# Second block's attention: low key parts and compressed values on all 128 rows, value products alternating by column half

## The chip, the core and the metric

The kernel runs on one core of one Trainium2 chip. The metric is the device time of one execution in microseconds (us). A core has five engines that run side by side and wait for each other through semaphores: PE (TensorE, matrix products; PEld is its weight load), DVE (VectorE), ACT (ScalarE), POOL (GpSimd) and SP, whose queue issues most of the loads. A matrix product has a stationary operand (the weights, up to 128 rows by 128 columns) and a moving operand of N columns that streams past it; the result goes to PSUM. A product may use a part of the array only: here "64\*128" in a row of the profile is a product on 64 rows of the array (a contraction over 64), "128\*64" one on all rows and one half of the columns (a result of 64 channels, in the lower or the upper half of the PSUM partitions), "32\*64" one on a quarter of the rows and half of the columns.

## The reference, cut to what matters

The kernel computes two blocks one after the other. The first (two layers of gated mixers and MLP, 512 tokens of x and 256 of a context) is the greater part of the time. The second block has eight heads of 64 channels in two groups, with three attentions per head that are added with gates: over compressed keys (31 of them), over selected blocks and over a window. With 512 tokens every block is selected and the window covers the sequence, so the last two are causal attentions with different keys and values. Four memory heads attend to 256 memory tokens beside them.

```python
s_c = einsum('bgrqd,bgnd->bgrqn', qb, k_c) * scale          # compressed
p_c = masked_softmax(s_c, c_mask); o_c = einsum('bgrqn,bgnd->bgrqd', p_c, v_c)
s_s = einsum('bgrqd,bgqkld->bgrqkl', qb, ks_g) * scale      # selected
o_s = einsum('bgrqkl,bgqkld->bgrqd', masked_softmax(s_s, s_mask), vs_g)
s_w = einsum('bgrqd,bgkd->bgrqk', qb, kw_blk) * scale       # window
o_w = einsum('bgrqk,bgkd->bgrqd', masked_softmax(s_w, w_mask), vw_blk)
o = gb[..., 0:1] * o_c + gb[..., 1:2] * o_s + gb[..., 2:3] * o_w
s_m = einsum('bshd,bmhd->bhsm', mq, mk) * scale             # memory
o_m = einsum('bhsm,bmhd->bshd', softmax(s_m), mv)
```

## The kernel before

Channels lie on the 128 partitions and tokens along the columns. Most products are made in a fast format (float32r) from numbers split in a high and a low part: high times high, plus the two mixed products. A product in full float32 (value products, transposes aside) is two passes of PE.

The program is recorded first. `Recorder` takes every instruction with the regions it touches; `schedule` (line 226) is a list scheduler that gives each engine its next instruction by priority (the place in the program) and readiness, by estimated durations (`cost`, line 191), and places the buffers; line 358 then issues everything in that order. So every row of the profile has the line L358, and instructions are told apart by the buffers they name: `pd` (projections), `pm` (scores, transposes) and `pa` (value products) are PSUM, with 3, 4 and 1 buffers; `slot` is a large SBUF row, `tmp` a scratch row, `wr`, `wh` and `wl` a loaded weight tile and its high and low parts, `const` what stays for good. The order on each engine is fixed when the program is built; on the chip an engine that waits holds up all that stands behind it.

The attention of the second block (`block2`, line 1570) comes after projections of keys, values and queries. A tile of queries `i` (0 to 3) holds two heads, one for each group `g`; head `g` has the rows 64g to 64g+63. `split_q` (line 1586) puts the high part of a head's queries on its own 64 rows and the low part on the other 64. The keys' high part `khi` is copied to both halves of the rows (ACT), so that one product of 128 rows gives high times high plus low times high. The keys' low part `klo` (line 1606) lies on the head's own 64 rows only.

A unit is (i, tb), tb being a block of 128 tokens; i = 0 to 3, tb = 3, 2, 1, 0. `nsa_scores` (line 1786) makes for each of two branches `br` and two groups `g`: a product with `khi` on 128 rows, a product with `klo` on 64 rows, and the causal mask added by a bf16 product with the identity, all of N = 512, 384, 256 or 256 columns (the mask 128); then DVE takes the maximum and ACT the exponential. `nsa_values` (line 1813) transposes each map in blocks of 128 (PE into `pm`), copies them to `tmp` (ACT for br 0, DVE for br 1), multiplies them with the values (`pa`, 128\*64, N = 128), and adds the compressed attention by one product per head with `vc`, which lies on 32 rows per token block (32\*64). One head is done before the other. Memory units (`mem_scores`, `mem_values`, lines 1842 and 1861) do the same for a pair of memory heads, with keys in `mem.khi` and `mem.klo` (line 1835, filled by `mem_keys`) and value products of N = 256. They stand after the second tile of queries. Between the units stand the projections and the output tiles of the list `beside` (line 1912): each is a stretch of 128\*128 products, `pd<-slot,wh` and `pd<-slot,wl`.

Before the attention the compressed keys and values are made: `psv` (line 1668) is a PSUM tile with the compressed values four times, once per quarter of the partitions, by 32-column products, and one ACT copy takes it to `vc`.

Elsewhere, `onesD` holds a matrix of 1/1024 and one of 1/256 for means (`csum`, `rstd`), the rope tables are loaded into a slot of their own (`rope_load`), and `mem_norm` (line 1544) loads the memory tokens into two slots.

Of the kernel before, what the change touches and what calls it, by code (L numbers as in the profile page):

```python
# [13 lines left out]
F32 = mybir.dt.float32  # L14
# [30 lines left out]
class View:  # L45
    """A region of a buffer that gets its place only when the order of the instructions is known."""
# [90 lines left out]
class Recorder:  # L137
    """Takes the program as it is written, orders each engine's instructions by priority and readiness with
    estimated durations, places the buffers, and then issues everything in that order."""
# [86 lines left out]
    def schedule(self):  # L226
        """List scheduling. A buffer's kind is served in program order."""
# [32 lines left out]
        def place(o):  # L260
            """places the buffers that the instruction is the first to touch, if they are all to be had"""
# [99 lines left out]
def tile_net(tc: tile.TileContext, A, out):  # L361
# [13 lines left out]
    def ld(o, i):  # L375
        sp.dma_start(out=o, in_=i)
# [28 lines left out]
    onesD = const([P, 2, P], F32)  # L405
    vec.memset(onesD[:, 0], 1.0 / 1024)
    vec.memset(onesD[:, 1], 1.0 / 256)
# [9 lines left out]
    def csum(srcs, n, w=0):  # L417
        """the mean over the channels of some blocks, on every partition"""
        ps = pm()[:, :n]
        for i, x in enumerate(srcs):  # L420
            pe.matmul(ps, onesD[:, w], x, start=i == 0, stop=i == len(srcs) - 1)
        return ps

    def rstd(ps, n):
        r = rst([P, TC])[:, :n]
        A_(r, ps, AF.Ln, bias=epst)
# [3 lines left out]
    def add_square(acc, o, sl, n, first):  # L430
        """adds the squares of a block to a tile of sums"""
# [51 lines left out]
    def run(blocks, acts, evac, order=R8, nk=None):  # L483
        """blocks: (key, source, groups); one weight tile after the other, all its tokens"""
# [5 lines left out]
    def narrow(src, acts, groups, evac):  # L490
        """a block of 32 columns: its high and low parts side by side, their products in two sets of rows"""
# [15 lines left out]
    def run_outer(blocks, acts, evac, groups, done=None, order=R8, ready=(), before=None):  # L507
        """as run, but group by group over a few resident weight tiles"""
# [55 lines left out]
    def pre(l, kind):  # L564
        """the gain and shift before the mixers (0) or the MLP (2), by conditioning"""
# [9 lines left out]
    def modulate(r, g, hs, gs, rs):  # L575
        """the next input of the matrix products: r * rs * gain + shift, in the two parts, r as four pairs of blocks"""
# [23 lines left out]
    def rms(r, n):  # L600
        ps = pm()[:, :n]
        for p in range(4):
# [3 lines left out]
            pe.matmul(ps, onesD[:, 0], q[:, 0], start=p == 0, stop=p == 3)  # L606
# [16 lines left out]
    def post_chain(g, o_, qs, old, hs, gs, gain=None):  # L623
        """the residual plus norm(o), kept in o's place and in DRAM, then the next norm"""
# [19 lines left out]
    def pairs():  # L644
        """activations in two parts: four tiles of [part, block of the pair, token]"""
# [26 lines left out]
    def rope_tables():  # L672
        """the cosines and signed sines by position, kept in DRAM until the second block"""
# [64 lines left out]
    def rows_of_three():  # L738
        """rows of the tokens of x, three to a slot"""
# [9 lines left out]
    class Later:  # L749
        """the tokens of x alone, by their place among all"""  # L750
# [7 lines left out]
    def gates(S, GX):  # L758
# [26 lines left out]
        # each head has two rows: the first of them takes the high part, the second the low one  # L785
# [46 lines left out]
    def mixers(l, hs, back, steps):  # L832
# [6 lines left out]
        # Fourier input and half of the conv module's  # L839
# [11 lines left out]
        # Fourier mixing: the sums over pairs of tokens s and n - s feed the cosines, the differences the sines,  # L851
# [1233 lines left out]
```

## Time and profile before

| | us |
|---|---|
| median of three runs | 2059.37 |
| lowest and highest of them | 2058.71, 2061.32 |
| the profiled execution, first to last instruction (span) | 2061.5 |

| engine | busy us | share of the span | instructions |
|---|---|---|---|
| PE | 1965.2 | 95% | 12772 |
| DVE | 1386.3 | 67% | 2380 |
| ACT | 878.3 | 43% | 1699 |
| POOL | 501.9 | 24% | 486 |

The span of the profiled execution is 2.1 us longer than the median of the runs, so the two agree within 0.1%. The attention with what runs beside it fills the stretch from 1785 to 2044 us of the span; the last 14 us finish the output. In the lists of the profile a matmul's duration contains its way through the array, which overlaps with the next one; what a product costs is the distance from its start to the next start.

### The profile page before, as it was taken

Reading aid. Unit: us, or ns where it says so; the run is one execution under the profiler, and the core shown is the slowest. Engines: PE = TensorE matmul, PEld = TensorE weight load, DVE = VectorE, ACT = ScalarE, POOL = GpSimd, SP = SyncE. Lnnn points to the kernel's source line nnn. Section 1 sums busy time; section 2 is a strip of 40 time slices with the busy share of each in tenths; the row PEclk is TensorE's granted clock in tenths of the full one; section 3 lists DMA queues with packets and bytes.
Section 4 is the critical chain, followed back from the end, with each engine's and each line's share of the span. In section 5 each row is a group of like instructions: output and inputs, shape, how many; then the busy total and the mean of one; then the engine's idle time right before and its main releaser. Section 6 shows DMA issues by size and latency. Waiting matters only on the chain.

```text
span 2061.5 us, 32412 instructions
## 1 busy us (share of the span) xinstructions
PE 1965.2 (95%) x12772; PEld 1672.1 (81%) x12772; DVE 1386.3 (67%) x2380; ACT 878.3 (43%) x1699; POOL 501.9 (24%) x486
## 2 busy tenths in 40 slices
PE   5999998988999999999899998899999998999999
PEld 3978885877988999999788886788989897776676
DVE  6588677287545665566878775887787785465664
ACT  4433355454322332234543355544343464553442
POOL 2210141245211222113320051542232232111210
PEclk8999998999999999999999999999999999999999
DMA  8233335251433221122321234322323342200201
GB/s 296 89 106 104 122 129 185 76 185 52 132 104 123 72 73 41 62 83 103 118 84 52 72 134 164 103 82 93 113 83 123 117 162 81 83 31 32 79 26 59
DMA packets 82570, 207.47 MB, mean 101 GB/s; under 512 B 8945, under 2 KB 36849, under 8 KB 82418
## 3 DMA queue, kind: packets, MB, share of 16 engines
q1 hardware_dynamic: 66690, 189.13, 27.0%
q10 hardware_dynamic: 15728, 16.27, 2.3%
q8 instruction: 100, 1.64, 0.3%
q14 instruction: 52, 0.43, 0.1%
HBM read 189.12 MB, written 16.25 MB: 100 GB/s over the span
## 4 chain that ended last, share of the span: by engine, by line
PE 65%; DVE 8%; issue 2%; ACT 1%; POOL 1%; DMA 1%; DVEq 0%; POOLq 0%; ACTq 0%
PE pd L358 44%; PE pm L358 18%; DVE slot L358 5%; PE pa L358 4%; DVE tmp L358 2%; DVE wl L358 1%; POOL slot L358 1%; ACT slot L358 0%; DMA wr<-in_w_ada 0%; ACT tmp L358 0%; ACT rs L358 0%; ACT wh L358 0%; DVE small L358 0%; POOL ftmp L358 0%; DMA wr<-in_w_in 0%
## 5 line engine op out<-in xcount | busy, mean ns | idle before, releaser
L358 PE MATMUL pd<-slot,wh 128*128 128x256 f32 (+2 forms) x4384 | 1092.2, 341 | 18.4 <-DVE slot L358 12.4
L358 PEld LDWEIGHTS pd<-slot,wh 128*128 128x128 f32 (+1 forms) x4384 | 745.1, 189 | 127.6 <-issue 18.7
L358 PE MATMUL pd<-slot,wl 128*128 128x256 f32 (+1 forms) x2136 | 724.1, 340 | 5.8 <-DVE wl L358 5.6
L358 PEld LDWEIGHTS pd<-slot,wl 128*128 128x128 f32 x2136 | 406.8, 191 | 55.0 <-DVE wl L358 7.7
L358 ACT ACTIVATE wh<-wr 128x1024 fp32r<-128x1024 f32 (+2 forms) x202 | 205.0, 1015 | 425.0 <-PE pd L358 388.1
L358 DVE TENSOR_TENSOR wl<-wr,wh 128x1024 fp32r<-128x1024 f32 (+2 forms) x199 | 248.4, 1248 | 129.1 <-ACT wh L358 128.2
L358 PE MATMUL pm<-slot,slot 128*128 128x256 f32 (+4 forms) x1674 | 256.7, 297 | 2.1 <-DVE tmp L358 1.6
L358 PEld LDWEIGHTS pm<-slot,slot 128*128 128x128 f32 (+1 forms) x1674 | 216.7, 191 | 28.2 <-issue 14.4
L358 DVE TENSOR_TENSOR slot<-pd,slot 128x512 f32<-128x512 f32 (+1 forms) x208 | 119.4, 574 | 127.0 <-PE pd L358 124.4
L358 PE MATMUL pd<-slot,slot 128*128 128x256 f32 (+1 forms) x1048 | 146.9, 289 | 2.9 <-ACT slot L358 2.6
L358 PEld LDWEIGHTS pd<-slot,slot 128*128 128x128 f32 x1048 | 132.8, 191 | 7.6 <-ACT slot L358 3.8
L358 DVE TENSOR_TENSOR slot<-ftmp,slot 128x512 fp32r<-128x512 f32 (+2 forms) x116 | 93.5, 809 | 36.1 <-POOL ftmp L358 34.5
L358 ACT ACTIVATE tmp<-tmp 128x512 f32<-128x512 f32 (+3 forms) x122 | 62.2, 545 | 126.9 <-DVE tmp L358 125.8
L358 DVE SCALAR_TENSOR_TENSOR slot<-slot,const,slot 128x512 f32<-128x512 f32 (+2 forms) x184 | 113.2, 664 | 0.8
L358 POOL TENSOR_TENSOR ftmp<-tmp 128x512 f32<-128x512 f32 x54 | 58.5, 1104 | 214.5 <-ACT tmp L358 214.5
L358 POOL TENSOR_TENSOR wr<-wr 128x512 f32<-128x512 f32 x27 | 39.3, 1455 | 290.0 <-DVE wl L358 248.9
L358 POOL TENSOR_TENSOR ftmp<-ftmp 128x256 f32<-128x256 f32 (+1 forms) x72 | 66.1, 918 | 166.7 <-ACT ftmp L358 162.5
L358 ACT ACTIVATE slot<-tmp 128x512 fp32r<-128x512 f32 (+1 forms) x134 | 80.7, 628 | 58.8 <-DVE tmp L358 38.8
L358 DVE TENSOR_TENSOR slot<-wr,slot 128x512 fp32r<-128x512 f32 (+1 forms) x85 | 87.3, 1033 | 17.2 <-ACT slot L358 17.2
L358 PE MATMUL pm<-slot,wh 128*128 128x256 f32 x544 | 98.4, 281 | 0.0
L358 ACT ACTIVATE slot<-wr 128x512 fp32r<-128x512 f32 (+1 forms) x85 | 72.0, 855 | 44.7 <-POOL wr L358 22.4
L358 PEld LDWEIGHTS pm<-slot,wh 128*128 128x128 f32 x544 | 84.0, 188 | 2.8 <-issue 1.6
(202 smaller groups left out, 2478.2 us busy)
## 6 DMA issues: line engine op xcount, KB each, us to landing
wr<-in_w_mlp SPq DMA_DIRECT2D x128, 512.0 KB, 3.4
wr<-in_w_ada SPq DMA_DIRECT2D x80, 512.0 KB, 4.0
wr<-in_w_in SPq DMA_DIRECT2D x66, 512.0 KB, 3.3
dram<-slot ACTq DMA_DIRECT2D x52, 256.0 KB, 2.5
tmp<-dram SPq DMA_DIRECT2D x40, 256.0 KB, 3.8
slot<-in_w_ada SPq DMA_DIRECT2D x16, 512.0 KB, 10.1
wr<-in_w_out SPq DMA_DIRECT2D x16, 512.0 KB, 3.9
wr<-in_w_out SPq DMA_DIRECT2D x8, 384.0 KB, 2.9
```

The costliest lines, as they stand in the source:

```text
L358: o.fn(*[conv(x) for x in o.a], **{k: conv(x) for k, x in o.k.items()})
```

## The change

The low parts of the keys get the same two copies as the high ones: `klo[g][br]` (and `mem.klo[h]`) is written on both halves of the rows, by two DVE subtractions instead of one, and the product with it is made on 128 rows. A third `kh` slot holds what this needs. The compressed values `vc` get one zero-padded tile of 128 rows per token block (`memset` once, four ACT copies of 32 rows instead of one copy of 128), and their product is made on 128 rows and 64 columns. In `nsa_values` the loop over branches is now the outer one, both heads' maps are transposed and copied, and then the products go block by block with the two heads in turn; both compressed products come last. `mem_values` alternates likewise. The copy that ACT makes is now that of head 0 and DVE's that of head 1.

To make room, `onesD` keeps only the 1/1024 matrix; the convolution module's mean of 256 channels takes it with a factor of 4 (in a `scalar_tensor_tensor` in place of a `tensor_tensor`, and in the scale of the logarithm), and the rope tables go to free columns of two slots that are in use anyway, by two loads of half the size. The rest of the diff removes comments.

```diff
@@ nsa keys (block2)
-        kh = [slot([P, 3, TX], F32R) for _ in range(2)]
+        kh = [slot([P, 3, TX], F32R) for _ in range(3)]
         khi = [[kh[g][:, br] for br in range(2)] for g in range(2)]
-        klo = [kh[br][:, 2] for br in range(2)]
+        klo = [[kh[2][:, br] if g else kh[br][:, 2] for br in range(2)] for g in range(2)]
         for br in range(2):
             for g in range(2):
-                a, b = own(g)
-                A_(khi[g][br][a], dst[br][a], AF.Copy)
-                A_(khi[g][br][b], dst[br][a], AF.Copy)
-                vec.tensor_tensor(klo[br][a], dst[br][a], khi[g][br][a].bitcast(F32), op=ALU.subtract)
+                a = own(g)[0]
+                for rows in own(g):
+                    A_(khi[g][br][rows], dst[br][a], AF.Copy)
+                    vec.tensor_tensor(klo[g][br][rows], dst[br][a], khi[g][br][a].bitcast(F32), op=ALU.subtract)
@@ compressed values
-        vc = const([P, 2, 64], F32)
-        A_(vc, psv, AF.Copy)
+        vc = const([P, 4, 2, 64], F32)
+        vec.memset(vc, 0.0)
+        for j in range(4):
+            A_(vc[32 * j:32 * j + 32, j], psv[32 * j:32 * j + 32], AF.Copy)
@@ nsa_scores
-                    pe.matmul(pS[:, :M], qs[i][a, g, ts], klo[br][a, :M], start=False, stop=False)
+                    pe.matmul(pS[:, :M], qs[i][:, g, ts], klo[g][br][:, :M], start=False, stop=False)
@@ nsa_values
-            for g in range(2):
-                og = po[64 * g:64 * g + 64]
-                for br in range(2):
+            og = [po[64 * g:64 * g + 64] for g in range(2)]
+            for br in range(2):
+                pTs = []
+                for g in range(2):
                     u = 2 * g + br
                     pT = pm((P, 4, P))
                     for s in range(tb + 1):
                         pe.transpose(pT[:, s, :], Pt[u][:, s * P:(s + 1) * P], ident)
-                    pTs = tmp([P, 4, P])
-                    (vec.tensor_copy if u % 2 else act.copy)(pTs[:, :tb + 1], pT[:, :tb + 1])
-                    for s in range(tb + 1):
-                        pe.matmul(og, vv[:, br, s, 64 * g:64 * g + 64], pTs[:, s, :], start=br == 0 and s == 0, stop=False)
-                pe.matmul(og, vc[32 * tb:32 * tb + 32, g, :], pcT[i][32 * tb:32 * tb + 32, g, :], start=False, stop=True)
+                    t = tmp([P, 4, P])
+                    (vec.tensor_copy if g else act.copy)(t[:, :tb + 1], pT[:, :tb + 1])
+                    pTs.append(t)
+                for s in range(tb + 1):
+                    for g in range(2):
+                        pe.matmul(og[g], vv[:, br, s, 64 * g:64 * g + 64], pTs[g][:, s, :], start=br == 0 and s == 0, stop=False)
+            for g in range(2):
+                pe.matmul(og[g], vc[:, tb, g, :], pcT[i][:, g, :], start=False, stop=True)
@@ mem_scores, mem_values
-                    pe.matmul(pS[:, t, :], mqs[b][r, h, c0:c0 + P], mem.klo[r, b, :], start=False, stop=True)
+                    pe.matmul(pS[:, t, :], mqs[b][:, h, c0:c0 + P], mem.klo[h][:, b, :], start=False, stop=True)
-                for c in range(2):
-                    pe.matmul(po[64 * h:64 * h + 64], mv[:, c, b * P + 64 * h:b * P + 64 * h + 64], eT[:, c],
+                eTs.append(eT)
+            for c in range(2):
+                for h in range(2):
+                    pe.matmul(po[64 * h:64 * h + 64], mv[:, c, b * P + 64 * h:b * P + 64 * h + 64], eTs[h][:, c],
@@ rope tables
-        rt = slot([P, 2, TX])
-        ld(rt, ropes)
-        mem.rope = rt[:, 0], rt[:, 1]
+        for i in range(2):
+            ld(mem.rope[i], ropes[:, i])
+        mem.rope = cst2[:, 8 * P:], mem.place[0][:, 4:6].rearrange("p a n -> p (a n)")
```

Since a scheduler sets the order, three places show what it made of this. The numbers in a buffer's name only tell one use of a buffer from another.

PE, before, unit (2, 3) (third tile of queries, last 128 tokens): `tmp_2831`, `tmp_2832` are the copied maps of head 0, `tmp_2834`, `tmp_2836` those of head 1, `slot_2529` the values, `const_2553` is `vc`, `tmp_2811` the compressed probabilities.

```order
L358 MATMUL pa_2837_18868<-tmp_2831_18850,slot_2529_17200 64x128 [waits DVE_49]
L358 MATMUL pa_2837_18868<-tmp_2831_18850,slot_2529_17200 64x128 x3
L358 MATMUL pa_2837_18868<-tmp_2832_18852,slot_2529_17200 64x128 [waits DVE_49]
L358 MATMUL pa_2837_18868<-tmp_2832_18852,slot_2529_17200 64x128 x3
L358 MATMUL pa_2837_18868<-tmp_2811_18747,const_2553_17353 64x128
L358 MATMUL pa_2837_18868<-tmp_2834_18859,slot_2529_17200 64x128 [waits Activation_49]
L358 MATMUL pa_2837_18868<-tmp_2834_18859,slot_2529_17200 64x128 x3
L358 MATMUL pa_2837_18868<-tmp_2836_18866,slot_2529_17200 64x128 [waits DVE_49]
L358 MATMUL pa_2837_18868<-tmp_2836_18866,slot_2529_17200 64x128 x3
L358 MATMUL pa_2837_18868<-tmp_2811_18747,const_2553_17353 64x128
```

The same unit after the change: `tmp_2831`, `tmp_2832` are now branch 0 of head 0 and head 1, `tmp_2834`, `tmp_2836` branch 1, `const_15` is `vc`.

```order
L358 MATMUL pa_2837_18878<-tmp_2831_18860,slot_2530_17205 64x128 [waits DVE_49]
L358 MATMUL pa_2837_18878<-tmp_2832_18862,slot_2530_17205 64x128 [waits DVE_49]
L358 MATMUL pa_2837_18878<-tmp_2831_18860,slot_2530_17205 64x128
L358 MATMUL pa_2837_18878<-tmp_2832_18862,slot_2530_17205 64x128
...
L358 MATMUL pa_2837_18878<-tmp_2834_18869,slot_2530_17205 64x128 [waits Activation_49]
L358 MATMUL pa_2837_18878<-tmp_2836_18876,slot_2530_17205 64x128 [waits DVE_49]
...
L358 MATMUL pa_2837_18878<-tmp_2811_18757,const_15_94 64x128 x2
```

The heads alternate product by product through the whole unit, and the two compressed products stand together at its end.

PE, unit (0, 3), before: `tmp_2598` and `tmp_2599` are branch 1 of head 0 and branch 0 of head 1; another stretch of head 1 follows later.

```order
L358 MATMUL pa_2600_17584<-tmp_2599_17582,slot_2529_17200 64x128 [waits Activation_49]
L358 MATMUL pa_2600_17584<-tmp_2598_17580,slot_2529_17200 64x128 [waits DVE_49]
L358 MATMUL pa_2600_17584<-tmp_2598_17580,slot_2529_17200 64x128 x3
L358 MATMUL pa_2600_17584<-tmp_2575_17464,const_2553_17353 64x128
L358 MATMUL pa_2600_17584<-tmp_2599_17582,slot_2529_17200 64x128 x3
```

The same place after: `tmp_2598` is head 1, `tmp_2599` head 0.

```order
L358 MATMUL pa_2600_17592<-tmp_2599_17590,slot_2530_17205 64x128 [waits Activation_49]
L358 MATMUL pa_2600_17592<-tmp_2598_17588,slot_2530_17205 64x128 [waits DVE_49]
L358 MATMUL pa_2600_17592<-tmp_2598_17588,slot_2530_17205 64x128 x3
L358 MATMUL pa_2600_17592<-tmp_2599_17590,slot_2530_17205 64x128 x3
L358 MATMUL pa_2600_17592<-tmp_2575_17472,const_15_94 64x128
```

Here each head's products still stand in a block, as its copy came ready.

PE at the compressed values, just ahead of the attention, before: `pm_2549` is the compressed keys' product, `pm_2550` is `psv`.

```order
L358 MATMUL pm_2549_17334<-small_2547_17327,slot_2342_16038 64x32 [waits DVE_49,PE_49]
L358 MATMUL pm_2549_17334<-small_2547_17327,slot_2342_16038 64x32 x3
L358 MATMUL pm_2550_17339<-slot_2342_16038,small_2547_17327 32x64 x8
L358 MATMUL pd_2543_17307<-slot_2456_16689,wh_2533_17225 128x512
L358 MATMUL pd_2543_17307<-slot_2450_16665,wl_2536_17236 128x512
```

After the change, with `pm_2551` as `psv`:

```order
L358 MATMUL pm_2550_17340<-small_2548_17333,slot_2343_16039 64x32 x3
L358 MATMUL pm_2551_17345<-slot_2343_16039,small_2548_17333 32x64 x4
L358 MATMUL pm_2551_17345<-slot_2343_16039,small_2548_17333 32x64 [waits Activation_49]
L358 MATMUL pm_2551_17345<-slot_2343_16039,small_2548_17333 32x64
L358 MATMUL pm_2551_17345<-slot_2343_16039,small_2548_17333 32x64 [waits Activation_49]
L358 MATMUL pm_2551_17345<-slot_2343_16039,small_2548_17333 32x64
L358 MATMUL pd_2544_17313<-slot_2456_16690,wh_2534_17231 128x512
```

The eight products of `psv` now have two waits for ACT among them: the third and the fourth quarter each wait for a copy out of the same PSUM tile.

## Rows read from the trace of the kernel before

**Rows 1.** The page: busy us (share) xinstructions; granted clock in 40 slices, tenths.
```profile
PE 1965.2 (95%) x12772; PEld 1672.1 (81%) x12772; DVE 1386.3 (67%) x2380; ACT 878.3 (43%) x1699; POOL 501.9 (24%) x486
...
PEclk8999998999999999999999999999999999999999
```

**Rows 2.** Busy time by stretch, sum of 1785 to 2044: us, busy us by engine.
```profile
sum 259.00, PE 258.66 PEld 181.25 DVE 157.43 ACT 122.01 POOL 47.33; mean PE 43.11 PEld 30.21 DVE 26.24 ACT 20.34 POOL 7.89
```

**Rows 3.** What PE waited for, 1700 to 2062: us, times, longest.
```profile
PE pm L358 <- DVE tmp L358: 3.6, 3, 2.6
```

**Rows 4.** Timelines of PE, products of 128 rows: start us, us, what, count.
```profile
303.01 0.40 PE L358 MATMUL pd<-const,const 128*128 128x128 bf16 x4
303.22 0.47 PE L358 MATMUL pd<-slot,slot 104*128 104x512 f32 x1
303.54 0.40 PE L358 MATMUL pd<-const,const 128*128 128x128 bf16 x4
...
700.49 2.98 PE L358 MATMUL pm<-slot,slot 128*128 128x256 f32 x24
703.31 0.88 PE L358 MATMUL pd<-slot,slot 128*128 128x256 f32 x6
...
1804.62 0.62 PE L358 MATMUL pd<-slot,wh 128*128 128x512 f32 x2
1805.08 0.40 PE L358 MATMUL pd<-slot,wl 128*128 128x512 f32 x1
```

**Rows 5.** Timeline of PE: the last three scores of unit (0, 0).
```profile
1824.23 0.68 PE L358 MATMUL pm<-slot,slot 128*128 128x256 f32 x2
1824.84 0.23 PE L358 MATMUL pm<-const,const 128*128 128x128 bf16 x1
...
1826.17 0.70 PE L358 MATMUL pd<-slot,wh 128*128 128x512 f32 x2
```

**Rows 6.** Timeline of PE: the scores of the first memory unit, eight products.
```profile
1904.11 0.28 PE L358 MATMUL pm<-slot 128*128 128x256 f32 x1
...
1904.94 1.63 PE L358 MATMUL pm<-slot,slot 64*128 64x256 f32 x5
1906.51 1.09 PE L358 MATMUL pm<-const,slot 128*128 128x128 f32 x8
```

**Rows 7.** Timeline of PE: value products of unit (2, 3).
```profile
1967.92 1.96 PE L358 MATMUL pa<-tmp,slot 128*64 128x128 f32 x16
1969.81 0.43 PE L358 MATMUL pa<-tmp,const 32*64 32x128 f32 x2
1970.17 1.96 PE L358 MATMUL pa<-tmp,slot 128*64 128x128 f32 x16
...
1972.41 0.49 PE L358 MATMUL pd<-slot,wl 128*128 128x512 f32 x1
```

**Rows 8.** Timelines of PE: memory value products, one head, both; unit (3, 3).
```profile
1908.23 1.08 PE L358 MATMUL pa<-tmp,slot 128*64 128x256 f32 x4
...
1935.86 1.09 PE L358 MATMUL pa<-tmp,slot 128*64 128x256 f32 x8
...
2014.41 1.96 PE L358 MATMUL pa<-tmp,slot 128*64 128x128 f32 x20
```

**Rows 9.** Timeline of PE and ACT at the compressed values.
```profile
1783.02 0.45 PE L358 MATMUL pm<-slot,small 64*32 64x64 f32 x16
...
1783.56 0.28 ACT L358 ACTIVATE const<-pm 128x128 f32<-128x128 f32 x1 [0.21 <-PE pm L358]
```

**Rows 10.** Timeline of DVE at the keys' parts: bracket, idle time before.
```profile
1752.94 2.34 DVE L358 TENSOR_TENSOR slot<-slot,slot 64x512 fp32r<-64x512 f32 x3 [0.53 <-ACT slot L358]
```

**Rows 11.** Timeline of SP's queue around the loads for the second block.
```profile
1638.73 1.68 SPq L358 DMA_DIRECT2D slot<-in_memT  x2
1647.27 0.33 SPq L358 DMA_DIRECT2D wr<-in_w_mlp  x1
```

**Rows 12.** DVE by form, 1780 to 2045: busy us, mean ns; idle before.
```profile
L358 DVE COPY tmp<-pm 128x512 f32<-128x512 f32 x12 | 8.2, 685 | 5.8 <-PE pm L358 5.8
```

More of the change, by code (lines that the diff above doesn't have):

```diff
@@ L404, in tile_net @@
     vec.memset(ones, 1.0)
-    onesD = const([P, 2, P], F32)
-    vec.memset(onesD[:, 0], 1.0 / 1024)
-    vec.memset(onesD[:, 1], 1.0 / 256)
+    onesD = const([P, P], F32)
+    vec.memset(onesD, 1.0 / 1024)
     epst = const([P, 1], F32)
@@ L415, in tile_net, with csum, rstd @@
     ld(colt, A["col"])
-    def csum(srcs, n, w=0):
+    def csum(srcs, n):
         ps = pm()[:, :n]
         for i, x in enumerate(srcs):
-            pe.matmul(ps, onesD[:, w], x, start=i == 0, stop=i == len(srcs) - 1)
+            pe.matmul(ps, onesD, x, start=i == 0, stop=i == len(srcs) - 1)
         return ps
-    def rstd(ps, n):
+    def rstd(ps, n, scale=1.0):
         r = rst([P, TC])[:, :n]
-        A_(r, ps, AF.Ln, bias=epst)
+        A_(r, ps, AF.Ln, bias=epst, scale=scale)
         A_(r, r, AF.Exp, scale=-0.5)
@@ L605, in rms @@
             vec.tensor_tensor(q[:, 0], q[:, 0], q[:, 1], op=ALU.add)
-            pe.matmul(ps, onesD[:, 0], q[:, 0], start=p == 0, stop=p == 3)
+            pe.matmul(ps, onesD, q[:, 0], start=p == 0, stop=p == 3)
         return rstd(ps, n)
@@ L936, in conv_norm @@
                 pool.tensor_tensor(xs, x[0], x[1], op=ALU.add)
-                mb = csum([xs], n, 1)
+                mb = csum([xs], n)
                 qs = []
                 for f in range(2):
-                    vec.tensor_tensor(x[f], x[f], mb, op=ALU.subtract)
+                    vec.scalar_tensor_tensor(x[f], mb, -4.0, x[f], op0=ALU.mult, op1=ALU.add)
                     q = tmp([P, n])
@@ L1527, in early @@
     def early():
-        cst2 = slot([P, 8 * P])
+        cst2 = slot([P, 12 * P])
         perm, bd64 = cst2[:, 0:P], cst2[:, P:2 * P]
@@ L1542, in early @@
         mem_norm()
+        mem.rope = cst2[:, 8 * P:], mem.place[0][:, 4:6].rearrange("p a n -> p (a n)")
     def mem_norm():
-        mt = [slot([P, 4, TC]) for _ in range(2)]
+        mt = [slot([P, n, TC]) for n in (6, 4)]
         for a in range(2):
-            sp.dma_start(out=mt[a], in_=A["memT"][:, 4 * a:4 * a + 4])
+            sp.dma_start(out=mt[a][:, 0:4], in_=A["memT"][:, 4 * a:4 * a + 4])
         r = [mt[p // 2][:, 2 * (p % 2):2 * (p % 2) + 2, :] for p in range(4)]
@@ L1793, in nsa_scores @@
                     u = 2 * g + br
-                    a = own(g)[0]
                     pS = pm()
                     pe.matmul(pS[:, :M], qs[i][:, g, ts], khi[g][br][:, :M], start=True, stop=False)
-                    pe.matmul(pS[:, :M], qs[i][a, g, ts], klo[br][a, :M], start=False, stop=False)
+                    pe.matmul(pS[:, :M], qs[i][:, g, ts], klo[g][br][:, :M], start=False, stop=False)
                     pe.matmul(pS[:, tb * P:N], identb, mask[1], start=False, stop=True)
@@ L1834, in mem_keys @@
             mem.khi = [mqs[g][:, 2].rearrange("p (b n) -> p b n", b=2) for g in range(2)]
-            mem.klo = qs[1][:, 2].rearrange("p (b n) -> p b n", b=2)
+            mem.klo = [t[:, 2].rearrange("p (b n) -> p b n", b=2) for t in (kh[2], qs[1])]
             for g in range(2):
-                a, b = own(g)
-                for rows in (a, b):
+                a = own(g)[0]
+                for rows in own(g):
                     A_(mem.khi[g][rows], mk[a], AF.Copy)
-                vec.tensor_tensor(mem.klo[a], mk[a], mem.khi[g][a].bitcast(F32), op=ALU.subtract)
+                    vec.tensor_tensor(mem.klo[g][rows], mk[a], mem.khi[g][a].bitcast(F32), op=ALU.subtract)
         def mem_scores(b, t2):
@@ L1845, in mem_scores @@
             for h in range(2):
-                r = slice(64 * h, 64 * h + 64)
                 pS = pm((P, 2, TC))
@@ L1862, in mem_values @@
             po = pa((P, 2, P))
+            eTs = []
             for h in range(2):
```

2 lines of the change are left out of this document (1 added, 1 removed).

## The prediction, made before the changed kernel ran

> **What bounds the kernel now.** The page comes first: PE is busy for 95% of the span, no other engine over 67%, and the granted clock stands at its upper level of 2.4 GHz but for the first microseconds and one early slice [rows 1]. Next the stage that the change touches, 1785 to 2044 us: PE is busy for 258.7 of 259.0 us at clock 1.00, DVE for 157 (61%), ACT for 122 (47%) [rows 2]. A busy PE may still hide waits, so the list of PE's waits follows: from 1700 us on the longest sum is 3.6 us, in three waits [rows 3]. So PE bounds this stage, in its own order, and a microsecond of PE saved here is one off the end until another engine's work is late. What a product costs PE is read as the distance from start to start. Where all products use 128 rows and 128 columns this is 0.117 us for N = 256 ((703.31 − 700.49) / 24) and 0.23 us for N = 512 (0.46 / 2) [rows 4]. Around the products of the stage that use a part of the array it is more, and this is where the change works.
>
> **Low key parts.** In unit (0, 0) three scores in a row (each a high product on 128 rows, a low one on 64, and the mask) take 1826.17 − 1824.23 = 1.94 us, 0.647 each [rows 5]. Two products of N = 256 in one shape cost 2 × 0.117 = 0.235. For the mask, a bf16 product between two others, the nearest rows are four of them and one 512 product on 128 rows: 0.53 us from first to next group, less 0.23 for the long one leaves 0.30 [rows 4]; three of the four follow a like one at 0.057 ((0.40 − 0.23) / 3, the 0.23 being the mask's own length in rows 5), so one that pays both changes of format costs 0.13. I take 0.125. So 0.647 − 0.235 − 0.125 = 0.29 us of each score goes on going to 64 rows and back. It does not depend on N, since it is lost between products. The change makes all three products of one shape; 4 tiles × 4 token blocks × 4 = 64 scores give 64 × 0.29 = **18.6 us**. A memory unit has four such pairs and no mask: its eight products take 1906.51 − 1904.11 = 2.40 us [rows 6], in one shape 8 × 0.117 = 0.94, so 1.46 us per unit and **5.8 us** for four. The 0.117 is the price of a product of 128 rows, so the wider one costs nothing beyond it. Bounds of the first sum: 7 if the mask's price were the whole 0.30, 20 if it were 0.10.
>
> **Value products, one shape.** A pass of N = 128 on one half of the columns costs 0.109 us: 16 passes of unit (2, 3) run 1.96 us, the last one's own 0.27 taken off, plus 0.05 for the opening one [rows 7]. The compressed product on 32 rows comes 1969.81 − 1967.92 = 1.89 us after the first of 16, where 16 × 0.109 + 0.05 = 1.79 is used: 0.09 to change shape, and its first pass opens the shape again, 0.05; the next head starts 0.36 us after it for two passes of 0.109, 0.14 to return. In the built order of before, 32 such products are entered (0.14 each, 4.6 us) and 12 are followed by more products of the other head (0.14 each, 1.7 us). With 128 rows these go.
>
> **Value products, two halves.** The trace shows already what two halves do. One head of a memory unit runs four passes in 1.08 us, and eight passes of both heads, where the scheduler happened to put them next to each other, in 1.09 us; in unit (3, 3) twenty passes of which four belong to the other head take the 1.96 us of sixteen [rows 8]. The other half's passes are free. In both cases the program has the heads in blocks (M M N N and A A A A B B A A A A, each letter a call of two passes). For eight passes to take the time of four, the first N pass has to start beside the first M pass, ahead of the three M passes that stand before it. So I walked through the built order by this rule: a pass starts as soon as its half is free, past at most three passes of the other half. The attention over keys has 384 passes in 33 stretches, 6 of them hidden: 378 × 0.109 + 33 × 0.05 + 4.6 + 1.7 = 49.2 us. After, 36 stretches; tiles 0 and 1 mostly keep each head in blocks, tiles 2 and 3 alternate, and 281 passes are left on the longer half: 281 × 0.109 + 36 × 0.05 = 32.4 us. That saves 16.8 us; three more stretches cost about 0.27 each (0.09 in, 0.09 out and what follows late), 0.8, so **16.0 us**. The memory's value products save nothing: two units overlap already and the other two stay in separate stretches.
>
> On this the Trainium skill (TensorE: Matmul & The Clock Gate, Part 3, "What overlaps and what doesn't") says otherwise: matmuls start and end in program order, strictly first in, first out, with no reordering. The rows of M M N N speak against it, since in that order the third call could not begin before the second. By the page the same walk gives 35.8 us after instead of 32.4, and the two memory units that alternate lose 0.27 each, so the gain here would be 12 us and not 16; the time would be 2027.
>
> **What is added.** (1) The four ACT copies of `vc`. PE now waits twice inside the eight products of `psv`, and behind these stand the projection tile and all scores, in PE's order. Before, the copy started 0.09 us after the last product and took 0.28 [rows 9]; with the way back to PE and the product's own 0.22 a round is 0.6 to 0.85 us. Two rounds: **1.5 us lost**, 1.2 to 1.7. (2) DVE gets four more subtractions of 64x512 ahead of the scores and two in `mem_keys`, 0.69 to 0.78 us each [rows 10]. DVE sits idle 0.53 us ahead of the first three and more behind, so the weights' low part that stands next in its queue is not late; nothing on the path, and 3 us if that idle time were gone. (3) Two loads of 256 KB in place of one of 512 KB, further ahead in SP's queue. Nothing holds them and SP issues nothing for 6.9 us at that place [rows 11]: nothing. (4) The mean's `scalar_tensor_tensor`, one memset and the shorter `onesD`: the same counts on PE, in stages untouched otherwise; nothing, 0.5 us at most either way. (5) What comes to light. PE's 259 us shrink by 40, so DVE goes from 61% to 72% of the stage, ACT to 56%, and chains that were just in time come late. The stage's waits are some 4 us now [rows 3]; I take **2.7 us more**, from 0 (everything still covered) to 8 (0.25 us at each of 32 copies of the second head).
>
> **Sum.** 18.6 + 5.8 + 16.0 − 1.5 − 2.7 = 36.2 us. The profiled execution's span is 2061.5, 2.1 above the median of the runs; I take the saving off both: span 2025.3, measured **2023.2 us**, 1.8% less.
>
> **The rivals.**
> - The halves do not overlap for these two-pass products as they do in the memory units, say because the two heads' copies come from two engines at different times. Then 384 passes in series and 36 stretches take 43.7 us, only 4.7 us are saved after the extra stretches, and the time is 2059.4 − (36.2 − 11.3) = 2034.5. For it: the first two tiles do run in blocks for that very reason. Against: unit (3, 3) overlaps such passes now [rows 8].
> - The loss around the low product belongs to the mask's format and not to the rows. Then the first term is 7 and the time 2035. Against: the memory units have no mask and lose more per low product, 0.37 [rows 6].
> - PE waits for the second copy. Alternating needs both heads' maps before the second product; 32 groups of products stand behind two copies each, and DVE's copy of 512 columns takes 0.69 us [rows 12]. With 0.5 us lost per group 16 us go, 2039. From 1.2 us per group on the whole gain is gone, and the change is slower: at 1.5 us, 48 lost, 2071. Against: the scheduler puts scores and projection products ahead of them in the fences above, and DVE's idle time before its copies [rows 12] shows it waiting for PE, not PE for it.
>
> **How the numbers follow.** Forecast 80%; no overlap 6%; mask 4%; waiting for copies, but faster, 6%; slower by that wait 2%; within 0.2% (4 us, about what a measurement of this kernel tells from no change) 2%. The range: with no wait come to light (2.7), the mask at 0.10 (1.4 more) and the shorter rounds (0.3) 40.6 us go, 2018.8, and a reach past more than three passes would take some 1 us off that, so low is 2017.5; high, 2035, takes in the first two rivals. Faster 0.96, same 0.02, slower 0.02.
>
> **What would show it.** Scores of N = 256 that follow each other at 0.36 us; no row with 64\*128 in the stage; the 36 passes of unit (2, 3) done in 2.1 us instead of 4.5, with starts in pairs; 128\*64 stretches of one head in tiles 0 and 1 still at 0.109 per pass; two waits of PE for ACT near 1783. Distances of 0.6 us between scores would prove the first term wrong; alternating passes at 0.109 each the second; PE waiting for `tmp` by more than 10 us in all, the last.

## The result, and the profile after

| | before | after |
|---|---|---|
| median of four runs, same chip | 2060.35 us (2058.71 to 2062.38) | 2021.74 us (2020.81 to 2022.72) |
| profiled execution, span | 2061.5 us | 2020.9 us |

The ratio is 0.9825, 95% interval 0.9809 to 0.9842: 38.6 us less, where 36.2 were forecast.

The page of the changed kernel, to be held against [rows 1] (busy us, share, instructions; granted clock in tenths):

```profile
PE 1924.0 (95%) x12772; PEld 1658.1 (82%) x12772; DVE 1386.2 (69%) x2386; ACT 876.8 (43%) x1702; POOL 506.1 (25%) x486
...
PEclk8999999999999999999999999989999999999999
```

PE has lost 41.2 us of busy time with the same 12772 instructions. DVE has six more subtractions and ACT three more copies, and their busy times hardly move. The stage itself, 1785 to 2003 us of this span, against [rows 2]:

```profile
sum 218.00, PE 217.14 PEld 164.49 DVE 153.27 ACT 117.60 POOL 47.89; mean PE 217.14 PEld 164.49 DVE 153.27 ACT 117.60 POOL 47.89
```

PE is busy for 99.6% of it and DVE for 70%, so PE still bounds the stage. What PE waited for, 1700 to 2022 us (us, times, longest), against [rows 3]:

```profile
PE pm L358 <- DVE tmp L358: 2.9, 2, 2.6
PE pd L358 <- ACT slot L358: 1.9, 2, 1.7
PE pm L358 <- ACT const L358: 0.7, 2, 0.4
PE pm L358 <- ACT slot L358: 0.4, 1, 0.4
```

The first line was 3.6 before, and its 2.6 stands ahead of the stage, as does the 1.7 of the second line, which was there before, too. New in the stage are the third line (at the compressed values, below), the fourth, and 0.2 us of the second:

```profile
1872.61 0.40 PE L358 MATMUL pd<-slot,wl 128*128 128x512 f32 x1
1873.36 0.44 PE L358 MATMUL pm<-const,slot 128*128 128x128 f32 x2 [0.35 <-ACT slot L358]
...
1942.72 0.74 PE L358 MATMUL pd<-slot,wh 128*128 128x512 f32 x2 [0.18 <-ACT slot L358]
```

At 1873.36 a transposition waits for ACT's exponential, at 1942.72 a weight product for an operand that ACT writes. From the start of the product ahead of each it is 0.75 and 0.45 us, where such pairs otherwise have 0.23 to 0.32 and mostly 0.03: some 0.9 us lost in all. A wait for a second copy is not in the list, but there is one, in unit (2, 3), below.

The places of the forecast, on PE's timeline (start, duration, form, count). First scores of N = 256 one after the other, which answer [rows 5]:

```profile
1815.83 0.49 PE L358 MATMUL pm<-slot,slot 128*128 128x256 f32 x2
1816.16 0.23 PE L358 MATMUL pm<-const,const 128*128 128x128 bf16 x1
1816.20 0.48 PE L358 MATMUL pm<-slot,slot 128*128 128x256 f32 x2
1816.52 0.23 PE L358 MATMUL pm<-const,const 128*128 128x128 bf16 x1
1816.56 0.48 PE L358 MATMUL pm<-slot,slot 128*128 128x256 f32 x2
```

From 1815.83 to 1816.20 to 1816.56: 0.365 us per score, where it was 0.647. A memory unit, against [rows 6]:

```profile
1897.07 0.63 PE L358 MATMUL pm<-slot,slot 128*128 128x256 f32 x4
...
1898.01 1.02 PE L358 MATMUL pd<-ftmp,slot 128*128 128x512 f32 x2
```

Its eight products take 0.94 us instead of 2.40. The value products of unit (2, 3), against [rows 7]:

```profile
1944.87 2.22 PE L358 MATMUL pa<-tmp,slot 128*64 128x128 f32 x31
1946.82 0.27 PE L358 MATMUL pa<-tmp,const 128*64 128x128 f32 x1
...
1947.35 0.50 PE L358 MATMUL pd<-slot,wl 128*128 128x512 f32 x1
```

2.48 us instead of 4.49 for the same 36 passes; the walk had said 2.1. DVE's copy of head 1's map, and the weight load (PEld) of head 1's first pass:

```profile
1944.51 0.68 DVE L358 COPY tmp<-pm 128x512 f32<-128x512 f32 x1
1945.24 1.61 PEld L358 LDWEIGHTS pa<-tmp,slot 128*64 128x64 f32 x29 [0.17 <-DVE tmp L358]
```

Head 0's first pass starts at 1944.87, head 1's only at 1945.24, 0.05 us after the copy ends at 1945.19: 0.37 us of waiting for the second copy. PE's own list of waits leaves it out, because it counts PE as busy: head 0's second pass started at 1945.03 and lasts 0.27 us.

The compressed values, against [rows 9], with what PE waited for in brackets:

```profile
1776.47 0.42 PE L358 MATMUL pm<-slot,small 64*32 64x64 f32 x8
1777.27 0.41 PE L358 MATMUL pm<-slot,small 64*32 64x64 f32 x4 [0.38 <-ACT const L358]
1778.03 0.41 PE L358 MATMUL pm<-slot,small 64*32 64x64 f32 x4 [0.36 <-ACT const L358]
1778.37 0.50 PE L358 MATMUL pd<-slot,wh 128*128 128x512 f32 x1
```

Before, the product that follows was this one:

```profile
1783.40 0.50 PE L358 MATMUL pd<-slot,wh 128*128 128x512 f32 x1
```

From the first product to what follows it takes 1.90 us, where it was 1783.40 − 1783.02 = 0.38: 1.52 us lost.

### The profile page after: what moved, and what is told of

Its sections match the earlier page's. It is cut to its first block, busy times and chain, and to the rows that moved or that the text cites. A ratio compares the mean times of both kernels' runs of the same rounds, so it can differ in the third digit from the quotient of the medians.

```text
span 2020.9 us, 32418 instructions
## 1 busy us (share of the span) xinstructions
PE 1924.0 (95%) x12772; PEld 1658.1 (82%) x12772; DVE 1386.2 (69%) x2386; ACT 876.8 (43%) x1702; POOL 506.1 (25%) x486
## 4 chain that ended last, share of the span: by engine, by line
PE 64%; DVE 9%; issue 2%; ACT 1%; DMA 1%; POOL 1%; DVEq 0%; ACTq 0%; POOLq 0%
PE pd L358 45%; PE pm L358 17%; DVE slot L358 5%; PE pa L358 3%; DVE tmp L358 2%; DVE wl L358 1%; DMA wr<-in_w_ada 1%; POOL slot L358 0%; ACT slot L358 0%; DVE small L358 0%; ACT wh L358 0%; DVE ftmp L358 0%; ACT tmp L358 0%; ACT rs L358 0%; DMA wr<-in_w_in 0%
## 5 line engine op out<-in xcount | busy, mean ns | idle before, releaser
L358 PE MATMUL pm<-slot,slot 128*128 128x256 f32 (+3 forms) x1674 | 238.5, 293 | 2.1 <-DVE tmp L358 1.6
L358 PEld LDWEIGHTS pm<-slot,slot 128*128 128x128 f32 x1674 | 213.0, 192 | 13.7 <-issue 5.2
```

The lines of the kernel that those rows point to most:

```text
L358: o.fn(*[conv(x) for x in o.a], **{k: conv(x) for k, x in o.k.items()})
```

## How the experiments are read

Executions of one and the same kernel differ here by up to 10 us: 33 runs of the kernel before lie between 2053.2 and 2062.9. That would bury effects of 2 to 5 us. So two more numbers stand beside each median. **Stage** is the stretch of the profiled execution from the first product of the compressed values to the start of the last product of the kernel; all parts of the change but the room it needs act in it. For the kernel before it is 2057.51 − 1783.02 = 274.49 us, after 2016.79 − 1776.47 = 240.32. **Stretches** is the time of all value products in it, each from its first start to the next start of anything else. **At clock 0.979** is the median after each run's time is moved to one mean granted clock: over those 33 runs the time falls by 1.2 us for each 0.001 of clock (correlation −0.85). Each ratio is taken to runs of the kernel before on the same chip; the other numbers are also compared across the three chips of the experiments, on which the medians of the kernel before lie 1 us apart (2058.4 to 2059.4).

| kernel | median | at clock 0.979 | ratio to before, interval | stage | stretches |
|---|---|---|---|---|---|
| before | 2058.7 (33 runs) | 2059.2 | | 274.49 | 58.30 |
| after | 2021.7 | 2022.3 | 0.9825, 0.9809 to 0.9842 | 240.32 | 42.47 |
| e1 low parts alone | 2035.6 | 2037.7 | 0.9888, 0.9872 to 0.9904 | 252.80 | 58.45 |
| e2 compressed values alone, with e5's edit | 2048.3 | 2048.3 | 0.9952, 0.9938 to 0.9965 | 263.88 | 47.48 |
| e3 room alone | 2061.6 | 2060.2 | 1.0011, 1.0002 to 1.0020 | 277.65 | 58.30 |
| e4 after, heads not alternating | 2027.7 | 2027.5 | 0.9849, 0.9835 to 0.9863 | 243.63 | 47.63 |
| e5 after, no wait at the compressed values | 2020.5 | 2020.6 | 0.9814, 0.9796 to 0.9833 | 237.31 | 42.47 |
| e7 both copies first, heads in blocks | 2010.5 | 2010.7 | 0.9761, 0.9747 to 0.9774 | 226.96 | 33.51 |
| e8 both copies first, alternating | 2001.4 | 2006.8 | 0.9729, 0.9709 to 0.9748 | 222.53 | 29.07 |
| e9 as e8, one engine copies both | 2008.2 | 2008.1 | 0.9753, 0.9732 to 0.9775 | 223.09 | 29.26 |
| e8 again | 2007.8 | 2008.4 | 0.9756, 0.9736 to 0.9777 | 222.52 | 29.09 |
| e7 again | 2010.9 | 2011.7 | 0.9768, 0.9750 to 0.9786 | 226.93 | 33.52 |

## The experiments

**e1, the low key parts alone.** Kernel before with

```diff
-pe.matmul(pS[:, :M], qs[i][a, g, ts], klo[br][a, :M], ...)
+pe.matmul(pS[:, :M], qs[i][:, g, ts], klo[g][br][:, :M], ...)
-pe.matmul(pS[:, t, :], mqs[b][r, h, c0:c0 + P], mem.klo[r, b, :], ...)
+pe.matmul(pS[:, t, :], mqs[b][:, h, c0:c0 + P], mem.klo[h][:, b, :], ...)
```

and the second copies of the low parts.

> The kernel before with the low key parts on 128 rows (64 key scores and the four memory units) and with the rope tables moved to make the room for them; value products, compressed values and the matrices of the means as before. Theory (the rows are what costs): 64 x 0.29 + 4 x 1.46 = 24.4 us less than before, 2035 to 2037 us, and scores of N = 256 that follow each other at 0.36 us. Rival (the loss belongs to the mask's format): the key scores give 7 us instead of 18.6, about 13 us less in all, 2047. If chains behind PE come late already here, up to 3 us of the 24.4 are missing.

The stage shrinks by 21.7 us, the time at clock 0.979 by 21.5. From start to next start the 64 key scores take 29.6 us instead of 47.0 (the changed kernel: 29.8) and the 32 memory products 4.6 instead of 10.0: 22.9 us. The rival, the mask's format, is out: it would have given 13. Of the other 1.2 us, 0.9 come back in two waits for ACT that the kernel before does not have and the changed kernel has, too (here at 1869.66 and 1940.65, idle 0.36 and 0.18 us): the chains behind PE come late already here, as the expectation had allowed for. The rest stays open.

**e2, the compressed values alone**, with the edit of e5 (below) against the waits. The heads stay in the order of before.

```diff
-pe.matmul(og, vc[32 * tb:32 * tb + 32, g, :], pcT[i][32 * tb:32 * tb + 32, g, :], ...)
+pe.matmul(og, vc[:, tb, g, :], pcT[i][:, g, :], ...)
```

> The kernel before with the compressed values on 128 rows alone (with the smaller matrix of the means and the moved rope tables that make the room), the heads' products in the order of before, and the four copies of the compressed values made to wait until all eight products of their tile are done, so that PE does not wait between them. Theory: the changes of shape around the 32 compressed products go (6.3 us) and, with all products in one shape, the head that follows starts up to three passes early: by the walk through the built order the value products' stretches shrink from 54.7 us to 43.6, 11 us less, 2049 us. Rival (strictly in program order, nothing starts early): the stretches shrink to 49.4, 5 to 7 us less, 2053 to 2055.

The stage gives 10.6 us, the stretches 58.30 − 47.48 = 10.8; forecast 11, strict order 5 to 7. Unit (2, 3) of this kernel shows why. In the program it is 16 passes of head 0, its two compressed ones, 16 of head 1, its two:

```profile
1958.70 2.02 PE L358 MATMUL pa<-tmp,slot 128*64 128x128 f32 x18
1960.50 0.27 PE L358 MATMUL pa<-tmp,const 128*64 128x128 f32 x1
1960.55 0.27 PE L358 MATMUL pa<-tmp,slot 128*64 128x128 f32 x1
1960.61 0.27 PE L358 MATMUL pa<-tmp,const 128*64 128x128 f32 x1
1960.66 1.58 PE L358 MATMUL pa<-tmp,slot 128*64 128x128 f32 x13
...
1962.39 0.51 PE L358 MATMUL pd<-slot,wl 128*128 128x512 f32 x1
```

The first row counts 18 passes with the values, so two of head 1's have started ahead of head 0's compressed passes, which stand before them in the program, and a third one between these. The single starts show how far ahead that is. Head 1's first pass starts at 1960.283, 6 ns after head 0's fifteenth, and so ahead of three that stand before it: the sixteenth (1960.386) and the two compressed ones (1960.496 and 1960.605). That is three passes, as the walk had it, in a kernel in which nothing alternates.

**e3, only what makes the room** (one matrix for the means, the rope tables in free columns).

```diff
-vec.tensor_tensor(x[f], x[f], mb, op=ALU.subtract)
+vec.scalar_tensor_tensor(x[f], mb, -4.0, x[f], op0=ALU.mult, op1=ALU.add)
```

> The kernel before with only what makes the room: one matrix of the means instead of two, with the factor of 4 in the convolution's norm, and the rope tables in free columns of other slots. Theory: no difference, 2060 us within 1.5 either way. Rival (it is this part that gives the 6 to 7 us that the profile of the changed kernel is ahead before the attention begins): 2053 to 2056.

The median is 2061.6 us, 0.1% above before; the interval, 1.0002 to 1.0020, just leaves out no difference. At clock 0.979 it is 1 us. So this part costs a little or nothing, and it gives nothing. Its profiled execution reaches the compressed values 4.4 us ahead of that of before (the changed kernel's 6.6), but over all its runs nothing is gained, so that lead is no gain of this part. The stage is 3.2 us longer than before, with the value stretches and scores alike to 0.1 us; the projections have the difference, and there the clock dips twice. Busy us by stretch, the clock behind the engines:

```profile
1815.00:1820.00 5.00, 5.00 (x29) 3.05 (x27) 2.87 (x5) 2.95 (x5) 0.57 (x1) 1.00 0.00 0
1820.00:1825.00 5.00, 5.00 (x18) 3.59 (x18) 3.73 (x9) 3.33 (x10) 0.00 (x0) 0.71 0.32 105
1825.00:1830.00 5.00, 5.00 (x30) 3.81 (x28) 2.71 (x9) 3.01 (x9) 0.63 (x1) 0.95 0.00 0
```

PE was busy all the while. There is a second dip at 1972, and 3.2 us for the two make some 1.5 us for one.

**e4, the changed kernel without alternation.** `nsa_values` and `mem_values` have the loops of before, the compressed product its 128 rows.

> The changed kernel with the value products in the order of before (each head's branches and its compressed product on end, in the key and the memory units); low parts and compressed values stay on 128 rows. Theory (a pass starts up to three passes early, past those of the other half): the value stretches grow from 37.9 us to 43.6, 5 to 6 us more than the changed kernel, 2027 us. Rival (strictly in program order): they grow to 49.5, 11.5 us more, 2033. If alternation is worth nothing, because waits for the second copy give it back, 2022.

The median is 2027.7 us, and 2027.5 at clock 0.979, 5.2 above the changed kernel; the stretches are 5.2 us longer (47.63 against 42.47). In strict order it would have been 11.5. So of the 15.8 us that the value products gave, 58.30 − 47.63 = 10.7 are due to the one shape and the early starts that it allows (e2 has 10.8), and 5.2 to the new order. The small gain of the order has its reason in the built order, of which tiles 0 and 1 alternate little.

**e5, no wait at the compressed values.** The four copies of `vc` wait until all eight products are done:

```diff
-                pe.matmul(psv[32 * j:32 * j + 32, g, :], ...)
+                last = pe.matmul(psv[32 * j:32 * j + 32, g, :], ...)
-            A_(vc[32 * j:32 * j + 32, j], psv[32 * j:32 * j + 32], AF.Copy)
+            act.activation(vc[32 * j:32 * j + 32, j], psv[32 * j:32 * j + 32], AF.Copy, ..., after=last)
```

> The changed kernel, with the four copies of the compressed values made to wait until all eight products of their PSUM tile are done, so that PE has no wait among them. Theory: the eight products and what follows take 0.38 us again instead of 1.90, 1.5 us less than the changed kernel, 2020 us; the profile shows no wait of PE for ACT at that place. If the lower clock that followed these waits in one profile comes with them always, 1.3 us more go, 2019. Rival (hidden elsewhere): 2021.7, no difference.

The timeline of PE at that place:

```profile
1782.40 0.45 PE L358 MATMUL pm<-slot,small 64*32 64x64 f32 x16
1782.78 0.50 PE L358 MATMUL pd<-slot,wh 128*128 128x512 f32 x1
```

0.38 us as before the change. The stage is 3.0 us shorter than the changed kernel's: 1.52 of waits, and 1.5 of a clock dip that stands behind them there. Busy us of the changed kernel in 5 us ahead of, in and behind that dip:

```profile
1774.00:1779.00 5.00, 4.05 (x37) 2.84 (x35) 1.97 (x2) 2.15 (x9) 1.89 (x2) 1.00 0.29 105
1779.00:1784.00 5.00, 5.00 (x18) 3.87 (x17) 1.57 (x6) 1.36 (x4) 0.49 (x2) 0.66 0.00 0
1784.00:1789.00 5.00, 5.00 (x31) 4.31 (x30) 4.04 (x9) 3.36 (x7) 0.00 (x0) 1.00 0.30 107
```

PE idled for 0.95 of the first 5 us, and behind that its products run in part at the lower level, 1.2 GHz (granted clock 0.66 in the mean of 5 us). In e4 the same two waits are followed by no dip, so it does not always come with them. The medians differ by 1.3 us with intervals that overlap: the wait is shown by the trace, the gain in time is only in keeping with it.

**e8 and e7, both copies before the first product**, both with the edit of e5. The first product of each head also waits for the copy of the other one, in the key and the memory units, so that the scheduler cannot take one head ahead. In e8 the heads alternate, in e7 they stand in blocks.

```diff
-for s in range(tb + 1):
-    for g in range(2):
-        pe.matmul(og[g], vv[...], pTs[g][:, s, :], ...)
+for s in range(tb + 1):
+    for g in range(2):          # e7: these two loops in the other order
+        pe.matmul(og[g], vv[...], pTs[g][:, s, :], ..., after=None if s else cp[1 - g])
```

> The changed kernel without the waits at the compressed values, and with alternation forced everywhere: the first product of each head also waits for the other head's copy, in the key units and in the memory units, so that the scheduler cannot take one head's products ahead. 30 stretches instead of 42, all A B A B. Theory: the value stretches go from 37.9 us to 25.9, 12 fewer entries give 12 x 0.27 = 3.2, the waits at the compressed values 1.5: 16.7 us less than the changed kernel if no wait for a second copy comes to light, 2005 us; up to 8 us (0.25 at each of 32 groups) come back if they do, 2013. Rival (PE waits for the second copy, 0.5 us at each of 32 groups): all is given back, 2021.

> As the version that forces alternation (below), with the same waits for both heads' copies, but within each group all products of one head before those of the other (A A A A B B B B instead of A B A B A B A B; each letter is a call of two passes). Theory (a pass starts up to three passes early, past those of the other half): by the walk the value stretches take 30.2 us, 4.3 more than with alternation. Rival (strictly in program order): 43.4 against 31.3, 12 us more than with alternation.

e8 takes 14.8 us off e5's stage, 13.4 of them in the stretches, of which there are 30 instead of 42. Most of this is not the order: e7, with the heads in blocks, takes off 10.4 (237.31 − 226.96) by putting both heads into one stretch, and alternating adds 4.4. By its ratio (0.9729, again 0.9756) it beats both kernels of this case. The first full group of 16 passes in e8, and in e7 another group of 16:

```profile
1798.34 1.09 PE L358 MATMUL pa<-tmp,slot 128*64 128x128 f32 x16
1799.36 0.38 PE L358 MATMUL pm<-slot,slot 128*128 128x256 f32 x1
```

```profile
1805.22 1.58 PE L358 MATMUL pa<-tmp,slot 128*64 128x128 f32 x16
1806.73 0.38 PE L358 MATMUL pm<-slot,slot 128*128 128x256 f32 x1
```

1.02 us alternating, 1.51 in blocks; one behind the other, 16 × 0.109 = 1.74 us would be needed for the passes alone. Over the stage the blocks cost 4.4 us more than alternating (4.3 by the walk, 12 in strict order). But the medians of the two stood 9.1 us apart, so both ran once more.

> The version that forces alternation once more, unchanged, beside the blocks version on the same chip: their medians stood 9.1 us apart, their stretches from the compressed values to the last product 4.4. If the early stages differ from execution to execution only, the stretch is 222.5 us again within 1 and the median within 2000 to 2007.

> The blocks version once more, unchanged. If the 4.4 us of the stretch are the whole effect, the stretch is 227 us again within 1 and the median 3 to 6 us above that of the version with alternation; 8 or more if it is not.

The stages repeat to 0.03 us (222.53 and 222.52, 226.96 and 226.93). The medians of the second time are 3.1 apart; over both times e8's is 2007.7 (nine runs, 2001.1 to 2012.5) and e7's 2010.9 (nine runs). The 9.1 were 4.4 and the clock: three of e8's first four runs had a mean of 0.982 to 0.984, those of e7 0.978 to 0.981. e8's median came out 0.8 us above the 2007 that was named as the upper end.

**e9, both copies on one engine.** e8 with the copies of the key units split by branch, as before the change:

```diff
-cp.append((vec.tensor_copy if g else act.copy)(t[:, :tb + 1], pT[:, :tb + 1]))
+cp.append((vec.tensor_copy if br else act.copy)(t[:, :tb + 1], pT[:, :tb + 1]))
```

> The version that forces alternation, with both heads' copies of a branch made by one engine again (ACT for the first branch, DVE for the second), so that the second copy follows the first instead of running beside it. Theory (the scheduler has other PE work to put ahead of the products, so when the second copy comes hardly matters): within 2 us of that version in the stretch from the compressed values to the last product, whose length there was 222.5 us. Rival (the two engines side by side are what keeps PE from waiting): 0.5 us at each of 32 groups, 16 us more, and waits of PE for tmp of that size.

The stage is 223.09, 0.6 us more than e8, and the stretches are 0.2 us longer. PE's largest wait for `tmp` is one that the kernel before has, too [rows 3], and its 2.6 us stand ahead of the stage:

```profile
PE pm L358 <- DVE tmp L358: 3.6, 3, 2.6
```

A new wait, for ACT's `tmp`, is 0.2 us. PE has other work ahead of the products, and when the second copy comes hardly matters. Splitting the copies by head is not what makes the change work.

## Why the prediction was right, point by point

**The bound** was read rightly: PE was and is busy for over 99% of the stage [rows 2], and of the 38.6 us that its products gave (17.3, 5.5 and 15.8, below) 34.2 arrive at the end of the stage. The clock was read too kindly: a 9 in [rows 1] stands for nine tenths or more, and the mean over the span is 0.978; in the stage itself it was 1.00.

**Low key parts.** Forecast 18.6 and 5.8. Measured from start to start, before and after: key scores 47.0 to 29.8 us, 17.3 less or 0.27 each; memory 10.0 to 4.5, 5.5 less. The mechanism holds, and so does the 0.29 at every width, where the three products of a score stand one behind the other: the means fall from 0.877 to 0.589 us for N = 512, from 0.764 to 0.473 for 384 and from 0.662 to 0.375 for 256. The 1.3 us that are missing lie mostly with the scores that have another product between theirs (6 of 64 before, 9 after). For them the sum took 0.29 too, and in e1 those six give 0.17 each. The 0.36 us per score named beforehand were 0.365. That tells the mask's price too: 0.365 − 0.235 = 0.13, as taken.

**Value products.** Forecast 16.0, measured 58.30 − 42.47 = 15.8, memory included. The levels agree, too. The walk leaves out the way out of a stretch, 0.09 us (the last pass starts 0.20 us ahead of what follows it, and not 0.109). With it, for 39 stretches and 42, the 54.7 and 37.9 us of the expectations are 58.2 and 41.7. Of the 0.8 us that the changed kernel takes beyond that, 0.37 are unit (2, 3), where PE waited for DVE's copy. No other stretch of this kernel has such a gap between its passes. The Trainium skill (TensorE: Matmul & The Clock Gate, Part 3, "What overlaps and what doesn't") has matmuls start strictly in program order. The traces here do not agree: in e2's rows passes of head 1 started ahead of older ones. The time alone leaned to the walk, 2022 against 2027; e2, e4 and e7 decide it. With 0.09 for each of 39, 40 and 30 stretches the expectations' times are 47.1, 47.2 and 32.9 us by the walk and 52.9, 53.1 and 46.1 in strict order; measured are 47.48, 47.63 and 33.51.

**The wait at the compressed values.** Forecast 1.5 lost, measured 1.52, in two waits of 0.38 and 0.36 us and the way round each. It can be had back for one line (e5).

**What comes to light.** Forecast 2.7 us of new waits behind DVE and ACT. The kind was right, the size was not. Two new waits for ACT cost 0.9 us (1873.36 and 1942.72), and they come with the shorter scores: e1 has both, e2 and e3 have neither. The late second copy in unit (2, 3) costs 0.37 us more, counted with the value products. Some 0.5 us in transposes and weight products stays unexplained. That the term nevertheless comes out near its size is luck: 1.5 us of a clock dip, which nothing in the prediction had foreseen, stand in for the waits that did not come.

**Nothing for the rest** held nearly. DVE's eight subtractions run in a row, against [rows 10], and the stage shows no wait of PE for the weights' low part behind them:

```profile
1746.33 5.89 DVE L358 TENSOR_TENSOR slot<-slot,slot 64x512 fp32r<-64x512 f32 x8 [0.53 <-ACT slot L358]
```

e3 moves the time by 0.1%, 1 us at one clock, where 0.5 us at most had been named.

**The sum** in the stage: 17.3 + 5.5 + 15.8 − 1.5 − 1.4 − 1.5 = 34.2, which is 274.49 − 240.32. The 1.4 are what comes to light outside the value products (0.9 and 0.5), the last 1.5 are the dip; without it the sum is 35.7, forecast 36.2. The parts add up, too: e1's 21.7, e2's 10.6 and e4's 243.63 − (237.31 + 1.52) = 4.8, less 1.52 of waits, make 35.6. The spans differ by 40.6 because the profiled execution of before reached the stage 6.6 us later. That is no effect of the change: e8 reached it at 1773.28 us in one profile and at 1782.74 in the other. At one clock the difference is 2059.2 − 2022.3 = 36.9.

**The rivals.** No overlap of halves: out by e4 and e8. The mask: out by e1. Waiting for the second copy: it happens once in the changed kernel, for 0.37 us. As a cost of 16 us it is out by e9, and by e8, where every group waits for both copies and the time falls.

## What to carry to other kernels

In this kernel a product that left the shape of its neighbours on PE paid on the way out and back: 0.29 us for one on 64 rows among products of 128, at N = 256, 384 and 512 alike. Zero rows or a second copy of an operand took that away; the price that the stage shows are the 1.5 us of waits at the compressed values, which e5 gets back. Two chains of products that use different halves of the columns ran side by side where the program had them within three passes of each other. Where a scheduler decides the order, that has to be made a dependency (e8), since it otherwise takes whichever is ready first. Where differences of a few us are sought among runs that scatter by 10, look at the stretch of the trace that the change acts on: it repeated to hundredths, as long as no clock dip fell into it (e3's two dips put 3.2 us on it). And a list of waits is not all: a start can be late while the engine still counts as busy, as in unit (2, 3).

## What the runs showed of the hardware

Passes on one half of the columns started ahead of older passes of the other half, up to three (e2's rows). No row of before showed how far this goes with compressed products among them.

The granted clock falls at other places in each execution, also where PE has been busy without a gap (0.71 in 1820 to 1825 us of e3), at the same work that runs at 1.00 in other executions. Two profiles of the same kernel, e8 and e8 again, in 100 to 400 us:

```profile
100.00:400.00 300.00, 285.15 (x1927) 232.18 (x1926) 218.58 (x471) 130.86 (x289) 56.94 (x79) 0.98 0.38 124
```

```profile
100.00:400.00 300.00, 285.69 (x1882) 230.71 (x1881) 220.59 (x475) 128.56 (x283) 55.11 (x76) 0.95 0.37 122
```

As long busy, at clock 0.95 it has started 45 products fewer. Most of the scatter of the runs goes with these dips: a mean clock of 0.976 stands beside 2062.9 us for the kernel before, 0.984 beside 2053.2. What sets them off stays open.
